# A quarter of the next norm's input, turned by DMA instead of TensorE at the ends of three feed-forward stages

## The chip, the cores and the metric

The kernel runs on one core of one Trainium2 chip. Times are device microseconds of one execution, from start to end; the median of three runs of the kernel before is 1848.39 us.

The engines are called by the profile's names: PE (TensorE, matmul), PEld (its weight loads), DVE (VectorE), ACT (ScalarE), POOL (GpSimd) and SP (SyncE, which only issues DMAs here).

## The reference

Two layers, each with three residual steps, on a float32 input of 512 tokens by 1024 channels:

```
x = x + 1/2 * SwiGLU(RMSNorm(x))        # FFN 1, inner width 2816
x = x + W_o(g_na * NA(h) W_na + g_f * FNet(h) W_f),  h = RMSNorm(x)
x = x + 1/2 * SwiGLU(RMSNorm(x))        # FFN 2

rms_norm(x, g) = x * rsqrt(mean(x * x) + 1e-6) * g
swiglu(x, w_in, w_out): g, u = split(x @ w_in); (silu(g) * u) @ w_out
```

A last RMSNorm ends it. What matters here is the border between one step and the next: the next step's products need the new x with channels on the partitions, multiplied by the norm's gain g.

## The kernel before

**Products.** Every float32 product is made of three matmuls. A number is split into a high part in the reduced fp32r format and the low rest; PE computes high times high (line 521), high weight times low activation (522) and low weight times high activation (524). The weight products run in a Strassen scheme: seven products of half-size blocks, numbered m = 1 to 7, stand for eight.

**Weights.** One list of weight blocks is walked through the whole program. SP loads a block (`raw`, 128x1024 or 128x512, line 148), up to 8 blocks ahead. Where a product wants the sum of two blocks, POOL adds the second by an accumulating DMA (line 158) or DVE adds it (line 172). ACT makes the high part `whi` (lines 199 and 194), DVE the low part `wlo` (lines 202 and 195), two blocks ahead of PE, in three buffers each.

**The end of a feed-forward stage.** The down projection is a list of 21 products (m, c), where c = 0, 1, 2 is the chunk of the inner width: m = 1 for c = 0 to 2, then m = 2 for c = 0 to 2, then 5, 6, 7, 3 of c = 0, the same of c = 1 and of c = 2, and last m = 4 for c = 0 to 2. The index i of the loop counts these; so i = 6 is product 5 of chunk 0, i = 13 is product 3 of chunk 1, i = 14, 15, 16 and 17 are products 5, 6, 7 and 3 of chunk 2, and i = 18 to 20 are product 4. The activations of product m are `c<m>h` (ACT, line 332) and `c<m>l` (DVE, line 333); some are combined first (DVE, line 779). The weight blocks of one product are its granules (two or three). When a product is complete over its chunks, DVE adds it to a quarter of x (`update`, line 785), and ACT sums the squares of that quarter for the next norm (`junk`, line 395).

**The next norm's input.** x is divided into four quarters: channel half i by token half j. `nxt.quad(i, j)` turns one. PE turns eight blocks of 128x128 into two PSUM banks `tr` (line 433), ACT multiplies by the gain from PSUM into `xr` (line 436, four of 128x256) and makes the high part `xh` (line 437), DVE the low part `xl` (line 438). Quarter (0, 0) of x is final behind the last m = 2 product, at i = 5; before, it is turned at i = 6. Quarters (1, 1) and (0, 1) are turned behind product 4 of chunk 0, and (1, 0) in the next stage.

**Turning by DMA.** The kernel has another way, which it uses for the gate's result: `words_apart` writes the 16-bit halves of a float32 block apart (`zs`, line 357, two ACT instructions of 128x1024), `turned_words` turns them by one transposing DMA from SP (`zt`, line 363), and `joined_words` puts the halves together again (line 376, two ACT instructions).

**Order.** What ACT, DVE and PE run is ordered by the compiler's list scheduler, except in blocks marked as manual. SP and POOL issue in program order, and each waits at a DMA whose buffer or source is not ready.

Of the kernel before, what the change touches and what calls it, by code (L numbers as in the profile page):

```python
# [9 lines left out]
F32 = mybir.dt.float32  # L10
# [4 lines left out]
AF = mybir.ActivationFunctionType  # L15
# [5 lines left out]
T = 512  # L21
# [70 lines left out]
def encoder_kernel(  # L92
    ctx: ExitStack, tc: tile.TileContext, xin, xtr, wst, gains, gfin, gbias, bias_in, dft, chan, ident_in, rot, out
):
    nc = tc.nc
    V, S, G, PE = nc.vector, nc.scalar, nc.gpsimd, nc.tensor
# [7 lines left out]
    dp = ctx.enter_context(tc.tile_pool(name="dp", bufs=2, space=bass.MemoryType.DRAM))  # L104
# [3 lines left out]
    def nm(s):  # L108
        uid[0] += 1
        return f"{s}_{uid[0]}"  # L110

    def slot(dt=F32, s="k", shape=(4, 256)):
        return kp.tile([P, *shape], dt, tag="k", name=nm(s), bufs=23)
# [12 lines left out]
    x = cp.tile([P, TB, D], F32, tag="x", name="x")  # L126
# [12 lines left out]
    class Raw:  # L139
# [3 lines left out]
        def load(self, parts=1):  # L143
            if self.t is None:
                self.t = raw_pool[0](self.n)
                for c in range(0, self.n, self.n // parts):
                    cs = slice(c, c + self.n // parts)
                    nc.sync.dma_start(out=self.t[:, cs], in_=wst[GRAN_AT[self.key]][:, cs])
                if self.plus:
                    gate = held.get(self.key)  # L150
                    if isinstance(gate, list):
                        gate.append(self)
                    else:
                        with tc.issue_after(gate) if gate else nullcontext():
                            self.summed()
# [48 lines left out]
                G.dma_start(out=t, in_=wst[GRAN_AT[self.then]][:, 0:n], accum_op=ALU.add)  # L204
            self.out = (hi, lo)

    held = {}

    def stage_items():
        items, st = [], 0  # L210
# [72 lines left out]
    class Stream:  # L283
# [32 lines left out]
        def next(self, ahead=AHEAD):  # L316
            self.prep(self.pos + 1 + ahead)
            it = self.items[self.pos]
            self.pos += 1
            return it.out  # L320
# [9 lines left out]
    def split(hi, lo, src, scale=None):  # L330
        if scale is None:
            S.activation(hi, src, AF.Copy)
            V.tensor_tensor(lo, src, hi.bitcast(F32), ALU.subtract)
            return
        S.activation(hi, src, AF.Copy, scale=scale)
        V.scalar_tensor_tensor(lo, src, scale, hi.bitcast(F32), ALU.mult, ALU.subtract)
# [15 lines left out]
    def words_apart(z):  # L352

        s = slot(U16, "zs", (2, 4, 2, P))
        words = z.bitcast(U16).rearrange("p b (q f h) -> p h q b f", q=4, h=2)
        for h in range(2):
            S.activation(s[:, h], words[:, h], AF.Copy)  # L357
        return s

    def turned_words(s):  # L360

        t = slot(U16, "zt", (2, 4, 256))
        nc.sync.dma_start_transpose(
            out=t.rearrange("p h q (b t) -> p (h q b) t", b=2), in_=s.rearrange("p h q b f -> p (h q b f)")
        )
        return t

    def apart(z):

        return turned_words(words_apart(z))  # L370

    def joined_words(to, t):

        to = to.bitcast(U16).rearrange("p i (t w) -> p w i t", w=2)
        for w in range(2):
            S.activation(to[:, w], t[:, w], AF.Copy)  # L376

    class Norm:
# [43 lines left out]
        def quad_high(self, i, j):  # L422

            self.tiles(i)
            js = slice(j * 256, (j + 1) * 256)
            hq, lq = self.h[i][:, :, js], self.l[i][:, :, js]
            raw = self.raw[i, j] = slot(F32, "xr")
            for k2 in range(2):
                tr = bank("tr").rearrange("p (a b) -> p a b", a=2)
                for k in range(2):  # L430
                    d = (4 * i + 2 * k2 + k) * P
                    for b in range(2):
                        PE.transpose(tr[:, k, b * P : (b + 1) * P], x[:, 2 * j + b, d : d + P], ident)
                for k in range(2):
                    kt = 2 * k2 + k
                    S.activation(raw[:, kt, :], tr[:, k, :], AF.Copy, scale=self.gain(4 * i + kt))
            S.activation(hq, raw, AF.Copy)
            return lambda: V.tensor_tensor(lq, raw, hq.bitcast(F32), ALU.subtract)

        def gain(self, kt):  # L440
            c = self.idx * DT + kt
# [186 lines left out]
    def stage_ffn(norm, nxt, late):  # L628
# [320 lines left out]
        if late or nxt.mix:  # L949
            tc.keep_in_program_order(S.activation(small("sq", 1), ones, AF.Sqrt))  # L950
        ps = {}
        for i, (m, c, _) in enumerate(steps):
            make(i)
            if i:
                make(i + 1)
            key = {6: 1, 4: 7}.get(m, m)
            if key not in ps:
                ps[key] = pair(f"o{key}")
            if m == 4 and c == 0 and nxt.mix:
                make(i + 2)  # L960
                ws.finish_stage()
                swap_pools(1)
            product(
                ps[key], made.pop(i), list(range(len(CHUNK[0][c]))), c == 0 and m in (1, 2, 3, 5, 7), c == 2,
                m in (4, 6), by_block=late and i == len(steps) - 1,
            )
            if i == 0:
                settle_at()
            if i == 3:
                turned.reverse()  # L970
                joined()
            if i == 5:
                joined()
            if m == 4 and c == 0 and not late:
                with tc.manual_schedule(engines={mybir.EngineType.DVE, mybir.EngineType.Activation}):
                    make(i + 2)
                    nxt.quad(1, 1)
                    if nxt.mix:
                        nxt.low01 = nxt.quad_high(0, 1)
                    else:  # L980
                        nxt.quad(0, 1)
            make(i + 2)
            if i == 6 and not late:
                nxt.quad(0, 0)
            if m == 4 and c == (0 if late else 1):
                update(ps[1], 1, 0, 1)
            if m == 4 and c == 0 and late:
                gf[0] = slot(F32, "gf", (D,))
                nc.sync.dma_start(out=gf[0], in_=bass.AP(tensor=gfin.tensor, offset=gfin.offset, ap=[[0, P], [1, D]]))
                ready = nxt.inverses(2)  # L990
                next(ready)
                next(ready)
                ends = nxt.terms()
            if m == 4 and c == 1 and late:
                for _ in ready:
                    pass
            if c < 2:
                continue
            if m == 1:
                update(ps[1], 0, 0, -1)  # L1000
            elif m == 2:
                update(ps[2], 0, 0, 1)
                nxt.squares(0, 0)
            elif m == 5:
                update(ps[5], 0, 1, 1)
                update(ps[5], 1, 1, -1)
            elif m == 6:
                update(ps[1], 1, 1, 1)
            elif m == 7:
                update(ps[7], 1, 1, 1)  # L1010
                nxt.squares(1, 1)
            elif m == 3:
                update(ps[1], 0, 1, -1)
                update(ps[3], 0, 1, 1)
                nxt.squares(0, 1)
                if late:
                    make(i + 3)
            elif late:
                with (
                    tc.issue_after(ws.items[-1].last.ins),  # L1020
                    tc.manual_schedule(engines={mybir.EngineType.DVE, mybir.EngineType.Activation}),
                ):
                    gained(2, 0)
                    gained(2, 1)
                    scaled(nxt, 2)
                    root = [nxt.inverse(b, *ends[b]) for b in range(2)]
                    update(ps[7], 1, 0, 1, (0,))
                    nxt.squares(1, 0, (0,))
                    next(root[0])
                    gained(3, 0)  # L1030
                    gained(3, 1)
                    scaled(nxt, 3)
                    gained(0, 0)
                    gained(1, 0)
                    update(ps[7], 1, 0, 1, (1,))
                    nxt.squares(1, 0, (1,))
                    next(root[1])
                    next(root[0])
                    next(root[0])
                    half_scaled(nxt, 0, 0)  # L1040
                    whole(nxt, 0, 1)
                    next(root[1])
                    next(root[1])
                    half_scaled(nxt, 1, 0)
                    whole(nxt, 1, 1)
            else:
                update(ps[7], 1, 0, 1)
                if not nxt.mix:
                    nxt.squares(1, 0)
                nxt.later((1, 0))  # L1050
# [982 lines left out]
```

## Time and profile before

| | us |
|---|---|
| runs of the kernel, median (lowest to highest of 3) | 1848.39 (1848.32 to 1849.78) |
| the profiled execution, its own time | 1848.74 |
| its span in the trace | 1847.0 |
| granted TensorE clock, mean | 0.998 |

A row of the timeline gives start, duration, engine, line, operation, what it writes and reads, the shape, how many of the same kind follow one another, and in brackets how long the engine had been idle before it and what released it. Times of rows are from the span's start. A row of several instructions gives the time from the first's start to the last's end. The next instruction of ACT or DVE may start about 0.1 us before the end that the row shows, and matmuls overlap by more, so spans between starts are used for sums. The three changed ends lie at 220 to 330 us (layer 0, FFN 1), 815 to 925 us (layer 0, FFN 2) and 1136 to 1245 us (layer 1, FFN 1).

### The profile page before, as it was taken

What the parts mean: (1) busy time and instruction counts of PE and PEld (TensorE: products, weight loads), DVE (VectorE), ACT (ScalarE), POOL (GpSimd) and SP (SyncE); (2) the same over time, 40 slices, a digit from 0 to 9 for tenths busy, and PEclk for the clock granted to TensorE, in tenths of its full rate; (3) what the DMA queues carried; (4) which work ended last, traced back from release to release, by engine and by line L of the source; (5) the groups of instructions that cost most, each with busy time, mean ns of one, the idle gap of its engine ahead of it and who ended that gap; (6) DMA issues with size and microseconds to landing.
All of it is one profiled execution on the core that took longest, in us unless ns stands there. A gap on an engine that the chain in (4) does not pass through costs nothing.

```text
span 1847.0 us, 24568 instructions
## 1 busy us (share of the span) xinstructions
PE 1835.7 (99%) x8850; PEld 1529.2 (83%) x8850; DVE 1602.6 (87%) x1942; ACT 1312.3 (71%) x1777; POOL 175.6 (10%) x215
## 2 busy tenths in 40 slices
PE   9999999999999999999999999999999999999998
PEld 7888888888888888888888888888888888888886
DVE  7878899786989987789998888997869899887898
ACT  6777875668676777787666778766776776777865
POOL 0001011100111010001010100101001101010010
PEclk9999999999999999999999999999999999999999
DMA  9898798933896789879888897989258966888695
GB/s 300 227 231 223 192 271 267 230 118 121 232 234 178 182 207 239 206 208 279 249 194 212 228 221 194 282 283 214 69 182 212 232 173 180 230 218 219 197 278 159
DMA packets 198378, 395.72 MB, mean 214 GB/s; under 512 B 103856, under 2 KB 103984, under 8 KB 198256
## 3 DMA queue, kind: packets, MB, share of 16 engines
q1 hardware_dynamic: 168912, 294.23, 49.9%
q0 software_dynamic: 28912, 99.38, 30.1%
q8 instruction: 69, 1.13, 0.2%
q10 hardware_dynamic: 432, 0.55, 0.1%
q14 instruction: 53, 0.43, 0.1%
HBM read 367.88 MB, written 2.11 MB: 200 GB/s over the span
## 4 chain that ended last, share of the span: by engine, by line
PE 94%; DVE 3%; issue 1%; DMA 1%; ACT 0%; POOL 0%; SPq 0%; DVEq 0%; ACTq 0%; POOLq 0%
PE A L521 10%; PE A L524 10%; PE A L522 10%; PE o L524 6%; PE o L521 6%; PE o L522 6%; PE B L521 5%; PE B L522 5%; PE B L524 5%; PE ps L326 4%; PE ps L327 3%; PE ps L328 3%; PE C L521 3%; PE C L522 3%; PE C L524 3%
## 5 line engine op out<-in xcount | busy, mean ns | idle before, releaser
L202 DVE TENSOR_TENSOR wlo<-raw,whi 128x1024 fp32r<-128x1024 f32 (+1 forms) x532 | 630.9, 1196 | 174.4 <-ACT whi L199 173.5
L199 ACT ACTIVATE whi<-raw 128x1024 fp32r<-128x1024 f32 (+1 forms) x532 | 544.0, 1033 | 263.4 <-PE A L522 53.6
L158 POOL DMA_DIRECT2D raw<-in_wst_dram x166 | 145.1, 898 | 1283.1 <-DMA raw<-in_wst_dram 530.5
L172 DVE TENSOR_TENSOR raw<-raw,raw 128x1024 f32<-128x1024 f32 (+1 forms) x148 | 177.0, 1196 | 2.0
L522 PE MATMUL A<-whi,xl 128*128 128x512 f32 x400 | 155.7, 389 | 0.0
L521 PE MATMUL A<-whi,xh 128*128 128x512 f32 x400 | 155.7, 389 | 0.0
L376 ACT ACTIVATE at<-zt 128x1024 uint16<-128x1024 uint16 (+2 forms) x96 | 110.3, 1166 | 15.1 <-DMA zt<-zs 15.0
L194 ACT ACTIVATE whi<-raw 128x1024 fp32r<-128x1024 f32 (+1 forms) x83 | 85.3, 1034 | 45.8 <-issue 12.5
L524 PE MATMUL A<-wlo,xh 128*128 128x512 f32 x400 | 115.0, 389 | 0.0
L195 DVE SCALAR_TENSOR_TENSOR wlo<-raw,whi 128x1024 fp32r<-128x1024 f32 (+1 forms) x83 | 98.6, 1198 | 13.1 <-ACT whi L194 13.1
L524 PEld LDWEIGHTS A<-wlo,xh 128*128 128x128 f32 x400 | 75.1, 188 | 15.5
L522 PEld LDWEIGHTS A<-whi,xl 128*128 128x128 f32 x400 | 75.1, 188 | 15.4
L521 PEld LDWEIGHTS A<-whi,xh 128*128 128x128 f32 x400 | 75.1, 188 | 15.4
L521 PE MATMUL C<-whi,xh 128*128 128x512 f32 x208 | 81.1, 390 | 0.2 <-ACT whi L199 0.2
L522 PE MATMUL C<-whi,xl 128*128 128x512 f32 x208 | 81.0, 389 | 0.0
L522 PE MATMUL B<-whi,xl 128*128 128x512 f32 x208 | 81.0, 389 | 0.0
L521 PE MATMUL B<-whi,xh 128*128 128x512 f32 x208 | 80.9, 389 | 0.0
L357 ACT ACTIVATE zs<-th 128x1024 uint16<-128x1024 uint16 x80 | 79.5, 1042 | 1.0 <-DVE th L766 0.9
L759 ACT ACTIVATE th<-sn,rh 128x512 f32<-128x512 f32 x80 | 55.1, 716 | 35.0 <-DVE sn L596 34.2
L591 ACT ACTIVATE sn<-A 128x512 f32<-128x512 f32 x104 | 59.2, 585 | 24.2 <-PE A L524 24.2
L524 PE MATMUL C<-wlo,xh 128*128 128x512 f32 x208 | 59.8, 389 | 0.0
L524 PE MATMUL B<-wlo,xh 128*128 128x512 f32 x208 | 59.8, 389 | 0.0
(429 smaller groups left out, 4686.6 us busy)
## 6 DMA issues: line engine op xcount, KB each, us to landing
raw<-in_wst_dram SPq DMA_DIRECT2D x468, 512.0 KB, 6.1
raw<-in_wst_dram POOLq DMA_DIRECT2D x176, 512.0 KB, 8.0
bm<-in_bias_dram SPq DMA_DIRECT2D x16, 512.0 KB, 4.1
raw<-in_wst_dram SPq DMA_DIRECT2D x30, 256.0 KB, 4.5
x<-in_xin_dram SPq DMA_DIRECT2D x4, 512.0 KB, 10.2
raw<-in_wst_dram POOLq DMA_DIRECT2D x8, 256.0 KB, 8.2
dft<-in_dft_dram POOLq DMA_DIRECT2D x8, 256.0 KB, 10.6
gb<-in_gbias_dram SPq DMA_DIRECT2D x4, 512.0 KB, 9.2
```

Of the source, the lines that this page charges most:

```text
L158: G.dma_start(out=self.t, in_=wst[GRAN_AT[self.plus]][:, 0 : self.n], accum_op=ALU.add)
L172: V.tensor_tensor(self.raw.t, self.raw.t, self.add.t, ALU.add)
L194: S.activation(hi, t, AF.Copy, scale=-1.0)
L195: self.last = V.scalar_tensor_tensor(lo, t, -1.0, hi.bitcast(F32), ALU.mult, ALU.subtract)
L199: S.activation(hi[:, cs], t[:, cs], AF.Copy)
L202: self.last = V.tensor_tensor(lo[:, cs], t[:, cs], hi[:, cs].bitcast(F32), ALU.subtract)
L326: PE.matmul(ps, lh, rh, start=start, stop=False, skip_group_check=again)
L357: S.activation(s[:, h], words[:, h], AF.Copy)
L376: S.activation(to[:, w], t[:, w], AF.Copy)
L521: PE.matmul(ps, lh, rh, start=start, stop=False, skip_group_check=again)
L522: PE.matmul(ps, ll, rh, start=False, stop=False, skip_group_check=again)
L524: PE.matmul(ps, lh, rl, start=False, stop=stop, skip_group_check=again)
```

## The change

At the three ends that another stage's norm follows (not at the last one), quarter (0, 0) of x is no longer turned by PE at i = 6. A generator with four steps takes its place:

- i = 13: `words_apart` of the quarter, two ACT instructions.
- i = 14: a small DMA from SP, `seen`, that reads sixteen numbers of the weight block that POOL's newest accumulating DMA wrote, and so waits for it; behind it in SP's order, the transposing DMA.
- i = 16: `joined_words` into `xr`, two ACT instructions.
- i = 17: four in-place multiplications by the gain (ACT, line 460 of the changed kernel) and the split into `xh` (ACT) and `xl` (DVE).

```diff
@@ class Raw, load
                 if self.plus:
+                    newest_sum[0] = self
                     gate = held.get(self.key)
...
-    held = {}
+    held, newest_sum = {}, [None]
...
+    def behind(raw):
+
+        seen = dp.tile([16], F32, tag="seen", name=nm("seen"))
+        to = bass.AP(tensor=seen.tensor, offset=seen.offset, ap=[[16, 1], [1, 16]])
+        return tc.issue_after(nc.sync.dma_start(out=to, in_=raw.t[0:1, 0:16]).ins)
...
+        def turned_quad(self, i, j):
+
+            js = slice(j * 256, (j + 1) * 256)
+            s = words_apart(x[:, 2 * j : 2 * j + 2, i * T : (i + 1) * T])
+            yield
+            with behind(newest_sum[0]):
+                t = turned_words(s)
+            yield
+            self.tiles(i)
+            raw = self.raw[i, j] = slot(F32, "xr")
+            joined_words(raw, t)
+            yield
+            for k in range(4):
+                S.activation(raw[:, k, :], raw[:, k, :], AF.Copy, scale=self.gain(4 * i + k))
+            split(self.h[i][:, :, js], self.l[i][:, :, js], raw)
+            yield
...
         ps = {}
+        quad00 = nxt.turned_quad(0, 0)
         for i, (m, c, _) in enumerate(steps):
...
             make(i + 2)
-            if i == 6 and not late:
-                nxt.quad(0, 0)
+            if i in (13, 14, 16, 17) and not late:
+                next(quad00)
```

What the scheduler makes of it on ACT, at the end of layer 0, FFN 1, from the weight split of product 4, chunk 0, first granule, on. Before (`whi_2652` and `whi_2668` belong to chunk 0 of product 4, `whi_2702` and `whi_2706` to chunk 1, `whi_2710` to chunk 2):

```order
L199 ACTIVATE whi_2652<-raw_2493 128x1024
L332 ACTIVATE c4h_2685<-at_1814 128x1024
L199 ACTIVATE whi_2668<-raw_2517 128x512
L395 ACTIVATE junk_2648,ssq_181<-x 128x512
L395 ACTIVATE junk_2650,ssq_181<-x 128x512
L199 ACTIVATE whi_2702<-raw_2536 128x1024
L332 ACTIVATE c4h_2698<-at_2074 128x1024
L199 ACTIVATE whi_2706<-raw_2563 128x1024
L395 ACTIVATE junk_2693,ssq_181<-x 128x512
L199 ACTIVATE whi_2710<-raw_2581 128x1024
```

The same place of the changed kernel, where `whi_2645` and `whi_2661` belong to chunk 0 and `whi_2701` to chunk 1:

```order
L200 ACTIVATE whi_2645<-raw_2474 128x1024
L383 ACTIVATE xr_2636<-zt_2545 128x1024 x2
L402 ACTIVATE junk_2641,ssq_181<-x 128x512
L200 ACTIVATE whi_2661<-raw_2501 128x512
L402 ACTIVATE junk_2643,ssq_181<-x 128x512
L333 ACTIVATE c4h_2678<-at_1814 128x1024
L460 ACTIVATE xr_2636<-xr_2636,gn 128x256 x4
L333 ACTIVATE c4h_2697<-at_2074 128x1024
L333 ACTIVATE xh_2634<-xr_2636 128x4x256
L402 ACTIVATE junk_2692,ssq_181<-x 128x512
L402 ACTIVATE junk_2694,ssq_181<-x 128x512
L200 ACTIVATE whi_2701<-raw_2520 128x1024
```

The first weight split of chunk 1 stood five rows behind that of chunk 0; now the joins, the scalings, `xh` and both c4h are ahead of it. The end of layer 1, FFN 1, has the same row order. At the end of layer 0, FFN 2, the order differs. Before, from the split of product 3, chunk 2, second granule (`whi_8005`), on; `whi_8034` and `whi_8052` are product 4, chunk 0, and `whi_8084` is chunk 1:

```order
L199 ACTIVATE whi_8005<-raw_7725 128x1024
L199 ACTIVATE whi_8034<-raw_7871 128x1024
L332 ACTIVATE c4h_8069<-at_7194 128x1024
L199 ACTIVATE whi_8052<-raw_7895 128x512
L395 ACTIVATE junk_8028,ssq_5468<-x 128x512
L395 ACTIVATE junk_8030,ssq_5468<-x 128x512
L199 ACTIVATE whi_8084<-raw_7914 128x1024
```

And of the changed kernel, where `whi_7992` is that of product 3, `whi_8026` and `whi_8044` are product 4, chunk 0, and `whi_8082` is chunk 1:

```order
L200 ACTIVATE whi_7992<-raw_7705 128x1024
L383 ACTIVATE xr_8015<-zt_7922 128x1024 x2
L200 ACTIVATE whi_8026<-raw_7851 128x1024
L402 ACTIVATE junk_8020,ssq_5467<-x 128x512
L402 ACTIVATE junk_8022,ssq_5467<-x 128x512
L200 ACTIVATE whi_8044<-raw_7878 128x512
L333 ACTIVATE c4h_8061<-at_7193 128x1024
L460 ACTIVATE xr_8015<-xr_8015,gn 128x256 x4
L200 ACTIVATE whi_8082<-raw_7897 128x1024
L333 ACTIVATE xh_8013<-xr_8015 128x4x256
```

Here the split of chunk 1 (`whi_8082`) has only the joins and the scalings put ahead of it, and `xh` stays behind it.

On SP, at the end of layer 0, FFN 1, the rows before are loads alone:

```order
L148 DMA raw_2493<-in_wst_dram 128x1024
L148 DMA raw_2517<-in_wst_dram 128x512
L148 DMA raw_2536<-in_wst_dram 128x1024
L148 DMA raw_2563<-in_wst_dram 128x1024
L148 DMA raw_2581<-in_wst_dram 128x1024
```

In the changed kernel the small read and the transposing DMA stand between them (`raw_2474`, `raw_2501` and `raw_2520` are the three blocks of product 4 that are `raw_2493`, `raw_2517` and `raw_2536` above):

```order
L148 DMA raw_2474<-in_wst_dram 128x1024
L373 DMA seen_2543<-raw_2413 1x16
L148 DMA raw_2501<-in_wst_dram 128x512
L148 DMA raw_2520<-in_wst_dram 128x1024
L364 DMA_TRANSPOSE zt_2545<-zs_2498 128x16x128
L148 DMA raw_2551<-in_wst_dram 128x1024
L148 DMA raw_2569<-in_wst_dram 128x1024
```

So every load from `raw_2501` on now stands behind the read that waits for POOL's last accumulation, and from `raw_2551` on behind the transposing DMA too. On PE the eight transposes are gone at three places and nothing else is moved.

## The prediction

> **What bounds the kernel now.** I read the busy shares first, then the chain that ended last, then the rows of the removed work, and last the windows and timelines round one changed place.
>
> ```profile
> PE 1835.7 (99%) x8850; PEld 1529.2 (83%) x8850; DVE 1602.6 (87%) x1942; ACT 1312.3 (71%) x1777; POOL 175.6 (10%) x215
> PE 94%; DVE 3%; issue 1%; DMA 1%; ACT 0%; POOL 0%; SPq 0%; DVEq 0%; ACTq 0%; POOLq 0%
> L433 PE MATMUL tr<-ident,x x160: 270/272/273, 254.2 to 1535.3; 128*128 128x128 f32 x160
> 250.00:255.00 5.00, 5.00 (x29) 4.21 (x27) 5.00 (x9) 3.76 (x7) 1.05 (x2) 1.00 0.97 235
> 305.00:310.00 5.00, 4.79 (x21) 3.43 (x20) 5.00 (x6) 3.43 (x4) 0.11 (x1) 1.00 0.95 347
> ```
>
> TensorE is busy 99% of the span and carries 94% of the chain. So an instruction that leaves TensorE shortens the program, provided its next operands are there in time. The third row lists the transposes; the change removes 24 of those 160 (8 at each of three FFN ends). The last two rows are windows of the first FFN's end (window; its length; then the busy time of PE, PEld, DVE, ACT, POOL; clock; DMA share; GB/s). Behind the removed transposes PE is full at a granted clock of 1.00; but DVE is full as well, the DMA engines are at 0.97, and in 305 to 310 PE has lost 0.21 us. The other engines have hardly any cover there, so the change is not judged by PE's share alone.
>
> **What is removed.** In the first FFN's end:
>
> ```profile
> 253.97 0.39 PE L524 MATMUL o<-wlo,c5h 128*128 128x512 f32 x1
> 254.20 1.03 PE L433 MATMUL tr<-ident,x 128*128 128x128 f32 x8
> 254.99 0.49 PE L521 MATMUL o<-whi,c6h 128*128 128x512 f32 x1
> 255.31 0.40 PE L522 MATMUL o<-whi,c6l 128*128 128x512 f32 x1
> ```
>
> Products start every 0.23 us (253.97 to 254.20). Eight transposes hold the next product back by 254.99 - 254.20 = 0.79 us, and the product behind them takes 0.32 us until the next start, 0.09 too long. That is 0.88 us a place, 2.6 us for three, 0.14% of the run: **the whole possible gain is under the 0.2%** (3.7 us) that a measurement of this kernel can tell from no change.
>
> **Where the first gain goes.** At the first FFN's end the 0.88 us have to survive the stretch up to product 3 of chunk 2:
>
> ```profile
> 277.83 2.01 ACT L199 ACTIVATE whi<-raw 128x1024 fp32r<-128x1024 f32 x2 [1.75 <-DMA raw<-in_wst_dram]
> 278.93 1.22 DVE L202 TENSOR_TENSOR wlo<-raw,whi 128x1024 fp32r<-128x1024 f32 x1 [1.06 <-ACT whi L199]
> 307.64 1.21 PE L524 MATMUL o<-wlo,c3h 128*128 128x512 f32 x4 [0.21 <-DVE wlo L202]
> ```
>
> A weight lands late before 277.83, DVE starts again at 278.93 and has no gap from there on until PE waits for its wlo at 307.64. The same DVE work lies in that stretch after the change (the moved xl subtraction leaves it at the front, before the gap, and comes back behind it). So PE, 0.88 us ahead, waits 0.88 us longer at 307.64, unless the landing moves ahead too: a load starts when a buffer comes free, so by at most the same 0.88 us. I call that lead d, from 0 to 0.88 us, and take the middle, 0.45, since no row decides it.
>
> **What is added on ACT, and when.** The two cuts of x into 16-bit words (zs) cost little:
>
> ```profile
> L357 ACT ACTIVATE zs<-th x80: 1036/1042/1061, 70.4 to 1737.9; 128x1024 uint16<-128x1024 uint16 x80
> 287.97 1.04 ACT L199 ACTIVATE whi<-raw 128x1024 fp32r<-128x1024 f32 x1
> 290.49 1.06 ACT L199 ACTIVATE whi<-raw 128x1024 fp32r<-128x1024 f32 x1 [1.48 <-DVE raw L172]
> ```
>
> They are 2 x 1.04 us in the row order behind the whi of 287.97, where ACT idles 1.48 us waiting for DVE; the rest delays operands that DVE, full of older work, takes later. Cost: nothing. The dear part is where the rejoining, scaling and splitting stand. In ACT's rows of the first and third changed end, everything from the joined words to the split xh stands ahead of the first weight split (whi) of product 4, chunk 1. Before:
>
> ```profile
> 306.57 2.01 ACT L199 ACTIVATE whi<-raw 128x1024 fp32r<-128x1024 f32 x2 [2.81 <-DVE raw L172]
> 308.48 1.04 ACT L332 ACTIVATE c4h<-at 128x1024 fp32r<-128x1024 f32 x1
> 309.43 0.62 ACT L199 ACTIVATE whi<-raw 128x512 fp32r<-128x512 f32 x1
> 310.23 0.63 ACT L395 ACTIVATE junk<-x 128x512 bf16<-128x512 f32 x1 [0.18 <-DVE x L785]
> 310.86 0.61 ACT L395 ACTIVATE junk<-x 128x512 bf16<-128x512 f32 x1
> 311.47 1.05 ACT L199 ACTIVATE whi<-raw 128x1024 fp32r<-128x1024 f32 x1
> 312.42 1.04 ACT L332 ACTIVATE c4h<-at 128x1024 fp32r<-128x1024 f32 x1
> 317.36 0.49 PE L521 MATMUL o<-whi,c4h 128*128 128x512 f32 x1
> ```
>
> The whi of 311.47 ends at 312.52; PE uses it at 317.36, so it has 4.84 us to spare. Durations of the new rows, by the nearest rows of the same kind:
>
> ```profile
> 242.82 2.58 ACT L376 ACTIVATE at<-zt 128x1024 uint16<-128x1024 uint16 x2
> 245.25 1.04 ACT L199 ACTIVATE whi<-raw 128x1024 fp32r<-128x1024 f32 x1
> 913.17 1.54 ACT L436 ACTIVATE xr<-tr,gn 128x256 f32<-128x256 f32 x4
> 914.74 1.06 ACT L437 ACTIVATE xh<-xr 128x1024 fp32r<-128x1024 f32 x1
> 915.71 1.55 ACT L436 ACTIVATE xr<-tr,gn 128x256 f32<-128x256 f32 x4
> 917.14 1.08 ACT L199 ACTIVATE whi<-raw 128x1024 fp32r<-128x1024 f32 x1
> ```
>
> Start to start: two joins 2.43 us, four scalings 1.43 (915.71 to 917.14; 1.57 at 913.17), one xh 0.97. In-place scalings are not in the trace; these rows read PSUM and write the same shape, and I bound the four by 1.2 and 1.6. From 306.57 the changed order then gives: two whi 1.91, joins 2.43, junk 0.61, whi of 512 columns 0.62, junk 0.61, c4h 0.95, scalings 1.43, c4h 0.95, xh 0.97, two junk 1.22, and the whi itself 1.05; the sum is 12.75, so it ends at 319.3 - d instead of 312.5. PE waits from 317.36 to 319.3: **+1.95 - d** against before, whatever lead PE had. The same queue brings the c4h of chunk 1 to 312.8 from 308.5, and with it DVE's c4l, the x updates and PE's 16 transposes at 315.70, which stand ahead of that product; these come about a microsecond late and then fall inside the same wait.
>
> The third changed end (layer 1, FFN 1) has the same row order:
>
> ```profile
> 1221.60 2.01 ACT L199 ACTIVATE whi<-raw 128x1024 fp32r<-128x1024 f32 x2 [2.80 <-DVE raw L172]
> 1232.83 0.49 PE L521 MATMUL o<-whi,c4h 128*128 128x512 f32 x1
> ```
>
> 1221.60 + 12.75 = 1234.35 against 1232.83: **+1.5 - d**. In the second end (layer 0, FFN 2) the whi of product 4, chunk 1, stands ahead of xh and of two junks:
>
> ```profile
> 901.78 2.01 ACT L199 ACTIVATE whi<-raw 128x1024 fp32r<-128x1024 f32 x2 [2.81 <-DVE raw L172]
> 908.01 0.39 PE L521 MATMUL o<-whi,c4h 128*128 128x512 f32 x1
> 913.76 0.49 PE L521 MATMUL o<-whi,c4h 128*128 128x512 f32 x1
> ```
>
> From 901.78: whi 0.95, joins 2.43, whi of product 4 chunk 0 to 906.2 (PE wants it at 908.01 - 0.88 = 907.1), junks 1.22, whi 0.62, c4h 0.95, scalings 1.43, whi to 911.4 (PE wants it at 912.9). Both are in time, by 0.9 and 1.5 us, so the full **-0.88** stays.
>
> **The queues that are passed.** SP gets the small read `seen` behind the last accumulated weight, then two weight loads, then the transposing DMA. Nothing else joins POOL's queue.
>
> ```profile
> 297.66 1.06 ACT L199 ACTIVATE whi<-raw 128x1024 fp32r<-128x1024 f32 x1 [0.80 <-DMA raw<-in_wst_dram]
> L363 SPq DMA_TRANSPOSE zt<-zs x44: 1317/3365/5361, 72.5 to 1738.9; - x44
> DMA to landing us min/median/max: 3.2/5.5/7.4
> DMA to landing us min/median/max: 3.4/6.4/11.3
> ```
>
> The last accumulation has landed by 297.6 (first row). SP stands still until then, issues `seen`, two loads and the transpose by about 299, and the words land 3.2 to 7.4 us later (third row: the 44 transposes of the same tile size), at 302 to 306.5; ACT comes to the joins at 308.5. So the wait is hidden by 2 us or more. The loads behind `seen` land in 3.4 to 11.3 us (last row, SP's weight loads of 285 to 325), by 310 at worst, and the first is wanted at 309.43: cost nothing, to +1 if the worst falls there. The transposing issue itself holds SP for 1.3 to 5.4 us (second row), to 304; the load behind it, for the second weight of product 4, chunk 1, lands by 315.5, and ACT now comes to it at 319.
>
> A rule of the Trainium skill speaks against this swap. "VectorE: DVE Perf Modes", section "Rules for kernel authors", says to turn 128x128 blocks on TensorE where PSUM can be the destination and by the crossbar DMA otherwise, and its section on the three transpose paths gives 390 ns and 1309 ns a block. As an estimate from that page, 16 blocks in a row would be 20.9 us on the DMA. The trace disagrees in part: eight f32 transposes cost PE 0.88 us, and a DMA of 16 blocks lands within 7.4 us.
>
> **Sum.** Against the profiled execution's 1848.74 us (its span of 1847.0 and 1.74 around it): +1.95 - 0.88 + 1.5 - 2d = +2.6 - 2d, which is +2.6 with d = 0, +0.8 with d = 0.88 and +1.7 in the middle. That profiled run lies 0.35 us above the median 1848.39, so the median goes to about **1850.0**, with 1849 to 1851.5 as this case's own range (scalings at 1.2 or 1.6 move it by 0.5 at each FFN1 end).
>
> **The rivals.**
> - *The whole gain.* ACT's queue runs further ahead than I hold, or PE takes the late whi within its slack: 1848.39 - 2.6 = 1845.8. For it: PE is full almost everywhere. Against it: 12.75 us of queue against 10.8 us of room. Chance 0.12.
> - *The change does nothing for the end.* The freed 0.88 us turn into waits for weights at all three ends, and the longer queue is just covered: 1848.4. For it: in both windows above DVE is full. Against: at the second end PE and DVE showed no stall. Chance 0.10.
> - *Late words, slower.* The joins stand at the head of ACT's queue with every weight split behind them. From a landing of 9.9 us on (308.5 - 298.6), each microsecond is one more on PE at the first and third end, and at the second from 0.9 us later. At 11.3 us, the longest landing of SP in that stretch, this gives +1.4 and +1.4 and +0.5, with d = 0 a sum of +5.9: 1854.3; with half of that delay 1852.6. For it: the DMA engines are at 0.95 and more in the windows above, and the transpose stands behind the accumulation's landing, so it is late with it. Against: no transpose of 44 took over 7.4. Chance 0.18. A smaller form of it at d = 0 stays in my own case.
> - *A transpose whose blocks go one by one.* If each of the 16 blocks took 1.3 us, the shortest time that the row above gives for a whole transposing issue, the words would land 21 us behind 298.6, the joins would wait from 308.5 to 319.6, and each end would lose about 11 us more: 1882 to 1884. Against: the same 7.4 us. Chance 0.01. That is what the rule named above would make of it.
> - *More than the gain.* PE's lead also frees weight buffers earlier, and the stall of 0.21 and its like vanish: under 1844.7. Chance 0.04.
>
> **How the numbers follow.** My case has 0.55, the whole gain 0.12, nothing 0.10, late words and serial blocks 0.19, more than the gain 0.04. Faster by over 0.2% (under 1844.7): 0.05. Slower by over 0.2% (over 1852.1): 0.19. Within: 0.76. The range runs from the whole gain, 1845.8, to 1853.5, which takes in most of the late words' case; it leaves out 0.04 below and about 0.1 above. The likeliest number is 1850.0.
>
> **What the profile after would show.** Right: no tr row of eight behind product 5 of chunk 0; the word transposes land before ACT's joins, which have no wait for zt; at the first and third end, PE waits 1 to 2 us at the first product of product 4, chunk 1, released by ACT's whi, and none at the second. Wrong: ACT sits idle at the joins with zt as releaser (late words); PE shows no wait there and the ends come 0.9 us earlier each (whole gain); PE waits longer for wlo at product 3, but not at product 4 (nothing).

## The result, and the profile after

| | us |
|---|---|
| kernel before, median of 11 runs | 1848.34 (1846.98 to 1850.53) |
| changed kernel, median of 11 runs | 1853.08 (1851.36 to 1854.88) |
| ratio | 1.0025, 95% interval 1.0016 to 1.0034 |
| the changed kernel's profiled execution | 1854.1, span 1852.3 |

The change makes the kernel 4.7 us slower. Two executions far above all others (2635.82 us in experiment 4, 2479.87 us of the kernel before) are not in the ratios below. The page's busy times of the changed kernel:

```profile
PE 1837.0 (99%) x8826; PEld 1526.2 (82%) x8826; DVE 1602.9 (87%) x1942; ACT 1324.3 (71%) x1789; POOL 176.0 (10%) x215
```

PE has 24 matmuls fewer and DVE and POOL as many as before; ACT has 12 instructions and 12 us more. At the place of the first removal, PE's timeline is now without a break:

```profile
253.90 0.39 PE L548 MATMUL o<-wlo,c5h 128*128 128x512 f32 x1
254.12 0.39 PE L545 MATMUL o<-whi,c6h 128*128 128x512 f32 x1
```

PE's first removal is there; the loss comes later. ACT at the first end, from the weight splits of product 3 and product 4, chunk 0, to that of product 4, chunk 1:

```profile
305.26 2.01 ACT L200 ACTIVATE whi<-raw 128x1024 fp32r<-128x1024 f32 x2 [2.81 <-DVE raw L173]
307.17 2.58 ACT L383 ACTIVATE xr<-zt 128x1024 uint16<-128x1024 uint16 x2
309.61 0.60 ACT L402 ACTIVATE junk<-x 128x512 bf16<-128x512 f32 x1
...
312.30 1.69 ACT L460 ACTIVATE xr<-xr,gn 128x256 f32<-128x256 f32 x4
313.90 1.04 ACT L333 ACTIVATE c4h<-at 128x1024 fp32r<-128x1024 f32 x1
314.84 1.04 ACT L333 ACTIVATE xh<-xr 128x1024 fp32r<-128x1024 f32 x1
...
317.02 2.94 ACT L200 ACTIVATE whi<-raw 128x1024 fp32r<-128x1024 f32 x3
```

ACT has no idle time from 305.26 on: the last row's whi is late because it stands last in a full queue. The joins at 307.17 wait for nothing, so the words were in time. PE beside it:

```profile
314.40 2.08 PE L440 MATMUL tr<-ident,x 128*128 128x128 f32 x16
318.11 0.50 PE L545 MATMUL o<-whi,c4h 128*128 128x512 f32 x1 [1.62 <-ACT whi L200]
```

PE stands still for 1.62 us at the first product of product 4, chunk 1, and ACT's whi ends that. At the third end the same, and ahead of it more. ACT and PE there:

```profile
1191.39 1.06 ACT L200 ACTIVATE whi<-raw 128x1024 fp32r<-128x1024 f32 x1 [2.95 <-DMA raw<-in_wst_dram]
1195.16 2.01 ACT L200 ACTIVATE whi<-raw 128x1024 fp32r<-128x1024 f32 x2 [1.76 <-DMA raw<-in_wst_dram]
1223.89 2.00 ACT L200 ACTIVATE whi<-raw 128x1024 fp32r<-128x1024 f32 x2 [2.81 <-DVE raw L173]
1235.63 2.94 ACT L200 ACTIVATE whi<-raw 128x1024 fp32r<-128x1024 f32 x3
```

```profile
1224.96 1.20 PE L548 MATMUL o<-wlo,c3h 128*128 128x512 f32 x4 [0.67 <-DVE wlo L203]
1236.73 0.50 PE L545 MATMUL o<-whi,c4h 128*128 128x512 f32 x1 [1.62 <-ACT whi L200]
```

DVE's timeline of the third end shows what the two late weights of ACT's first rows did:

```profile
1192.48 1.23 DVE L203 TENSOR_TENSOR wlo<-raw,whi 128x1024 fp32r<-128x1024 f32 x1 [1.81 <-ACT whi L200]
1193.62 1.22 DVE L173 TENSOR_TENSOR raw<-raw,raw 128x1024 f32<-128x1024 f32 x1
1196.25 1.23 DVE L203 TENSOR_TENSOR wlo<-raw,whi 128x1024 fp32r<-128x1024 f32 x1 [1.42 <-ACT whi L200]
```

Before, DVE had no gap there. Now it idles 3.2 us, and the queue of ACT that begins with product 3's last split starts at 1223.89 instead of 1221.60.

At the second end, where the splits of chunk 1 stay ahead of xh, PE has no such wait:

```profile
911.06 1.04 ACT L200 ACTIVATE whi<-raw 128x1024 fp32r<-128x1024 f32 x1
912.01 1.04 ACT L333 ACTIVATE xh<-xr 128x1024 fp32r<-128x1024 f32 x1
```

It is not free of loss all the same: DVE waits for ACT's whi and c4h there (0.24 us ahead of 906.89, 0.25 us ahead of 909.58), and PE, behind DVE, gives back 0.83 us.

How far PE leads or lags the trace before is read by matching the same matmul in both and taking the difference of their starts (us, negative is ahead): the first matmul of product 4, chunk 1, at 317.36 before and at 318.11 here makes +0.75. "Start" is ahead of the first removal: what stands there is the scatter of two executions.

| execution | start | past removal 1 | product 4, c 0 | c 1 | next stage | ahead of end 2 | past removal 2 | past end 2 | past removal 3 | product 4, c 0 | c 1 | next stage | mixer's middle |
|---|---|---|---|---|---|---|---|---|---|---|---|---|---|
| changed | -0.07 | -1.01 | -1.29 | +0.75 | +0.74 | +0.17 | -0.76 | +0.07 | -0.90 | +1.87 | +3.93 | +3.93 | +5.56 |
| changed, second trace | -0.37 | -1.31 | -0.05 | +2.05 | +2.05 | +1.44 | +0.50 | +0.50 | -0.47 | +2.65 | +4.73 | +4.73 | +6.23 |

(The middle of the mixer is at 1350 us of the trace before; the second trace is an experiment below.) Each removal gives 0.93 or 0.94 us. The first end gives back 2 us at chunk 1 of product 4, the third end 2.8 to 3.1 us ahead of product 4 and 2.1 at it.

### The profile page after: what moved, and what is told of

The parts are those of the page before. It is cut to its first block, busy times and chain, and to the rows that moved or that the text cites. A ratio compares the mean times of both kernels' runs of the same rounds, so it can differ in the third digit from the quotient of the medians.

```text
span 1852.3 us, 24543 instructions
## 1 busy us (share of the span) xinstructions
PE 1837.0 (99%) x8826; PEld 1526.2 (82%) x8826; DVE 1602.9 (87%) x1942; ACT 1324.3 (71%) x1789; POOL 176.0 (10%) x215
```

## The experiments

Two theories. **Queue theory**: the loss is where the scheduler puts the added work on ACT (and DVE): weight splits stand behind it. **DMA theory**: the small read holds SP, and the transposing DMA takes time of the DMA engines, so weights are late. Times are medians; ratios are against the kernel before on the same chip.

**1. The split one step later.**

```diff
-            if i in (13, 14, 16, 17) and not late:
+            if i in (13, 14, 16, 18) and not late:
```

> The scaling and split of the turned quarter are issued at i = 18 instead of 17, so ACT makes the weight split of product 4, chunk 1, ahead of them; joins, words and DMAs stay. Queue theory (ACT's order at two ends, 1.9 and 2.1 us of PE wait on whi): those two waits vanish, the 2.7 us of wlo waits at the end of layer 1, FFN 1, stay: 1848.5 to 1849.5 us. DMA theory (the small read that holds SP and the transposing DMA make weights late): no change, 1852 to 1854 us.

Measured: 1857.75 us, ratio 1.0047 (1.0035 to 1.0060): slower still, which neither theory expected. The wait at product 4 is gone, and a larger one stands at the next stage's first products:

```profile
330.45 0.49 PE L545 MATMUL A<-whi,xh 128*128 128x512 f32 x1 [1.01 <-ACT xh L333]
331.83 0.50 PE L546 MATMUL A<-whi,xl 128*128 128x512 f32 x1 [0.88 <-DVE xl L334]
```

The scheduler now put xh behind the next stage's other quarter, and that stage begins with it. PE lost 4.1 us at the first and 4.0 us at the third of these borders. The two waits, with one matmul between them, are only 2.3 us of that (at 0.23 us a product the first was due at 329.28 and started at 330.45, the second was due at 330.68 and started at 331.83). Most of the rest is TensorE's clock. Windows of that trace:

```profile
331.00:332.00 1.00, 0.17 (x1) 0.17 (x2) 0.97 (x2) 1.00 (x2) 0.00 (x0) 1.00 1.03 422
333.00:334.00 1.00, 1.00 (x4) 0.78 (x3) 1.00 (x2) 0.93 (x1) 0.00 (x0) 0.50 1.02 410
337.00:338.00 1.00, 1.00 (x6) 0.84 (x5) 0.96 (x4) 0.13 (x1) 0.00 (x0) 1.00 0.00 0
```

Behind the waits PE is full, but the granted clock is 0.50 for about 3.4 us, which costs half of that, 1.7 us; products start every 0.43 us there (333.03, 333.45, 333.88). The third border shows the same, and so do both borders of experiment 3. Behind the single wait of 1.62 us for whi in the changed kernel the clock stays at 1.00. So 1.7 us at each border of experiments 1 and 3 are not waiting.

The place in ACT's queue sets the waits, and the work has a due time on both sides.

**2. DVE's order put back, ACT's left.** Product 4's combinations are issued where the kernel before runs them.

```diff
+        def four(c):
+            if c not in fours:
+                fours[c] = comb(part(1, 0, c), part(1, 0, c), part(0, 0, c), ALU.subtract)
+            return fours[c]
...
+            if i in {8: 0, 11: 1, 15: 2} and not late:
+                four({8: 0, 11: 1, 15: 2}[i])
```

> The changed kernel with only DVE's order put back: product 4's combinations of chunks 0, 1, 2 are issued at i = 8, 11, 15, where the kernel before runs them; scaling and split stay at i = 17. Queue theory: the ACT waits of about 2 us at both FFN 1 ends stay, the wlo waits at the end of layer 1, FFN 1, shrink from 2.7 to under 1: about 1851 us. DMA theory: 1852 to 1854 us.

Measured: 1851.86 us, ratio 1.0021 (1.0012 to 1.0030). The waits on whi stay (+2.1 us at both ends). At the third end PE lost 1.9 us ahead of product 4, against 2.8 and 3.1 in the two traces of the changed kernel: less, but not under 1. The intervals of this ratio and the changed kernel's overlap, so what the order of the combinations costs is not settled by time.

**3. Both.**

> Split at i = 18 and combinations pinned, all else as in the changed kernel. Queue theory: no wait of PE on whi at product 4 and hardly any on wlo, so most of 2.6 us of removed transposes stays: 1846 to 1847.5 us, faster than the kernel before. DMA theory: 1852 to 1854 us.

Measured: 1857.52 us, ratio 1.0047 (1.0034 to 1.0060), with the same waits for xh and xl and the same low clock as in the first (4.1 us in all at each border). Ahead of the first of them PE was 0.9 us ahead of its start and had kept the whole gain up to there.

**4. The words alone.** The quarter is still turned by PE; the cuts, the small read and the transposing DMA are issued, and the words are not used.

```diff
-            if i in (13, 14, 16, 17) and not late:
+            if i == 6 and not late:
+                nxt.quad(0, 0)
+            if i in (13, 14) and not late:
                 next(quad00)
```

> The kernel before with its quarter still turned by PE, and beside it the two word cuts on ACT, the small read and the transposing DMA of the change, whose result is not read. Queue theory: two ACT instructions in idle time, 1848 to 1849 us. DMA theory: the whole loss and the removed transposes besides, 1852 to 1856 us.

Measured: 1849.28 us, ratio 1.0003 (0.9994 to 1.0012). In its trace PE's lag is -0.4 us behind the first end and changes by no more than 0.1 us at the two others; between them, in layer 0's mixer, it moves by 0.5 us and back. The DMA theory, which put the whole loss here, falls: SP's halt and the transposing DMAs cost nothing that the trace shows, and at most 2.2 us by the interval.

**5. The split at its due place.** Scaling and split stand in the block that runs in program order behind product 4, chunk 0; once with the combinations pinned, once without.

```diff
                 with tc.manual_schedule(engines={mybir.EngineType.DVE, mybir.EngineType.Activation}):
+                    next(quad00)
                     make(i + 2)
                     nxt.quad(1, 1)
...
-            if i in (13, 14, 16, 17) and not late:
+            if i in (13, 14, 16) and not late:
                 next(quad00)
```

> Scaling and split of the turned quarter stand at the head of the block that runs in program order behind product 4 of chunk 0; ACT then makes both weight splits of chunk 1 and the first of chunk 2 ahead of them, and xh still ahead of the next stage's quarters. Combinations of product 4 pinned. Queue theory: no wait of PE on whi at product 4 and none on xh at the next stage's first product: 1846 to 1847.5 us. DMA theory (late weights): 1851 to 1854 us.

> The same without pinning the combinations. Queue theory: the ACT waits are gone; whatever DVE's later combinations cost stays at layer 1, FFN 1: 1847 to 1849 us, 1 to 2 us over the pinned one. If the combinations cost nothing: equal to the pinned one within 0.5 us. DMA theory: 1851 to 1854 us.

Measured: 1849.43 us, ratio 1.0002 (0.9994 to 1.0011), and 1849.29 us, ratio 1.0007 (0.9998 to 1.0016). ACT at the first end, pinned:

```profile
313.77 1.05 ACT L200 ACTIVATE whi<-raw 128x1024 fp32r<-128x1024 f32 x1
...
318.79 1.69 ACT L460 ACTIVATE xr<-xr,gn 128x256 f32<-128x256 f32 x4
320.51 1.06 ACT L333 ACTIVATE xh<-xr 128x1024 fp32r<-128x1024 f32 x1
```

The whi of chunk 1 is at 313.77 and PE waits for no whi at either end, nor for xh. The order on ACT was worth about 3.7 us, 1853.08 less 1849.4. But nothing is faster than before: the removed 2.8 us are not in the time. Pinned or not makes no difference here, so the combinations are not the cause of what is left.

**6. The removal alone.** ACT scales x itself, with no transposes, words or DMAs.

```diff
+                S.activation(raw[:, kt, :], v, AF.Copy, scale=self.gain(4 * i + kt))   # v: 128x256 of x
...
             if i == 6 and not late:
-                nxt.quad(0, 0)
+                nxt.quad_unturned(0, 0)
```

> The kernel before with the eight transposes of quarter (0, 0) left out at i = 6 at the three ends: ACT scales x itself into xr, so the turning is left out; no word, no DMA, no other order. It measures what the removal alone can give. Queue theory: 1845.8 to 1846.5 us (2.0 to 2.6 us less). If PE's lead is eaten by weights and DVE at every end: 1848 to 1848.7 us.

Measured: 1849.80 us, ratio 1.0005 (0.9996 to 1.0013). So even the bare removal gives nothing. Its trace: PE gains 0.94 us at each of the three places, and loses 0.7, 3.6 and 0.6 us again before the end of the stage. At the second end two weights are late, DVE stands still and PE then waits for it. ACT's rows, DVE's rows, then rows of the waits from 815 to 910 us (who waited for whom: us in total, times, longest; PEld's waits hold PE back too):

```profile
872.98 1.06 ACT L199 ACTIVATE whi<-raw 128x1024 fp32r<-128x1024 f32 x1 [3.52 <-DMA raw<-in_wst_dram]
876.83 1.06 ACT L199 ACTIVATE whi<-raw 128x1024 fp32r<-128x1024 f32 x1 [2.79 <-DMA raw<-in_wst_dram]
874.07 1.23 DVE L202 TENSOR_TENSOR wlo<-raw,whi 128x1024 fp32r<-128x1024 f32 x1 [3.34 <-PE o L532]
877.92 1.23 DVE L202 TENSOR_TENSOR wlo<-raw,whi 128x1024 fp32r<-128x1024 f32 x1 [1.49 <-ACT whi L199]
```

```profile
ACT whi L199 <- DMA raw<-in_wst_dram: 6.5, 3, 3.5
PEld o L534 <- DVE wlo L202: 3.5, 7, 1.1
PE o L534 <- DVE wlo L202: 0.7, 1, 0.7
```

The first DVE row names PE as its releaser, but ACT's whi, late by its load, ended at 874.04, just ahead of it. In this trace PE does not gain because DVE, once stopped by a late weight, has no slack up to product 3 of chunk 2; experiment 8 puts that to the test.

**7. The changed kernel once more**, for its trace.

> The changed kernel once more, for its trace. Queue theory: about 2 us of PE wait on whi at the first product of product 4, chunk 1, at both FFN 1 ends, as in the first trace. If the 2.7 us of wlo waits at layer 1, FFN 1, and the 1.4 us in the mixer behind it come from that execution alone, they are smaller or elsewhere here; if from the order, the wlo waits stay within 1 us.

Measured: 1856.38 us in one run. The PE waits on whi are 1.62 us again at the first end (PE then starts at 319.38), and the wlo waits and the mixer's loss come back (3.1 and 1.5 us, the table above). So they are not of one execution.

**8. Slack for DVE.** Two of DVE's weight additions an end are left out, in the kernel of experiment 5 (pinned), in the kernel before as a control, and in that without the transposes.

```diff
-                V.tensor_tensor(self.raw.t, self.raw.t, self.add.t, ALU.add)
+                if not self.unsummed:
+                    V.tensor_tensor(self.raw.t, self.raw.t, self.add.t, ALU.add)
...
                     add(d, None if dma else b)
+                    items[-1].unsummed = name("a") == "oa" and idx == 2
```

> The kernel of the pinned sums with the split inside the ordered block, and DVE's two weight additions of product 3, chunk 2, left out at the ends that make them on DVE (their weights are loaded but not added, so that part of the sum is left out). Theory that the removed transposes are lost because DVE, behind a late weight, has no slack up to product 3 of chunk 2: with 2.3 us less DVE work ahead of that product the lead of 0.9 us an end stays, 2 to 2.6 us under the control that leaves out the same additions in the kernel before. Theory that the gain goes elsewhere (ACT, the joins, the DMAs): within 0.7 us of that control.

> The control: the kernel before with the same two weight additions a stage left out. Its own waits at product 3 were 0.2 us at one end, so both theories expect 1847.5 to 1848.8 us.

> The control without the eight transposes at i = 6: ACT writes zeros of the same shape into xr, so the turning is left out, and so are the two weight additions. DVE theory: 2 to 2.6 us under the control. Other theory: within 0.7 us of it, as the removal alone was within 1 us of the kernel before.

Measured: 1846.43 us for the turn by DMA, 1847.38 for the control, 1846.14 for the removal alone; ratios against the kernel before 0.9991 (0.9982 to 1.0000), 0.9992 (0.9984 to 1.0001) and 0.9987 (0.9978 to 0.9996). The sizes, 0.95 and 1.24 us under the control, lie between the two expectations and inside the intervals. The traces tell more. PE's lead over the control's trace:

| execution | start | past removal 1 | end 1 over | past removal 2 | past end 3 | 1775 us | 1830 us |
|---|---|---|---|---|---|---|---|
| turn by DMA, no sums | +0.81 | -0.13 | -0.13 | -1.05 | -2.01 | -2.01 | -0.69 |
| removal alone, no sums | +0.26 | -0.68 | -0.68 | -0.76 | -1.62 | -1.64 | +0.68 |

With DVE's slack, nothing is lost at the three ends by these two traces: the first kernel goes from +0.81 to -2.01, all of 3 x 0.94; the second gains as much at each end and loses 0.9 us in a mixer between them. The third end shows the same across all traces. DVE's idle time there, from the removal to product 3 of chunk 2, beside what PE loses from behind the removal to product 4 (us):

| third end | DVE idle | PE loses |
|---|---|---|
| before; experiments 4 and 9 (turned by PE) | 0.0; 0.2, 0.2 | 0.0; 0.0, 0.0 |
| changed, first and second trace | 3.2, 3.3 | 2.8, 3.1 |
| experiments 1, 2, 3 | 1.7, 2.4, 1.2 | 1.2, 1.9, 0.7 |
| experiment 5, pinned and not | 2.4, 1.8 | 1.9, 1.3 |
| removal alone (6) | 1.1 | 0.6 |
| no sums: turn by DMA, removal alone | 1.4, 1.9 | 0.0, 0.0 |

In every trace without the transposes and with DVE's additions PE loses DVE's idle time less 0.2 to 0.6 us, and where DVE has 2.3 us less to do, stops of 1.4 and 1.9 us cost nothing. The slack differs by end: at the second, DVE idles 2.6 us in the changed kernel's first trace and PE loses only 0.1 us up to product 4. So the DVE theory holds at these ends. But 1.3 and 2.3 us are lost at the last FFN's end, which was not changed. ACT and DVE there, in the removal alone, and the window of that end:

```profile
1785.35 1.06 ACT L201 ACTIVATE whi<-raw 128x1024 fp32r<-128x1024 f32 x1 [3.45 <-DMA raw<-in_wst_dram]
1786.44 1.23 DVE L204 TENSOR_TENSOR wlo<-raw,whi 128x1024 fp32r<-128x1024 f32 x1 [2.31 <-ACT whi L201]
1790.06 1.23 DVE L204 TENSOR_TENSOR wlo<-raw,whi 128x1024 fp32r<-128x1024 f32 x1 [1.26 <-ACT whi L201]
```

```profile
1765.00:1815.00 50.00, 49.10 (x212) 39.11 (x211) 45.78 (x46) 26.05 (x28) 7.80 (x9) 1.00 1.02 281
```

PE has lost 0.9 us in these 50, where the control loses none, again behind late weights. That the lead itself causes this is not shown: with PE's transposes kept at the third end the lag against the kernel before moves from 1775 to 1830 us by +0.6 (experiment 4), -0.8 (the control) and -0.8 us (experiment 9), so part of it is scatter.

**9. One end only.** The turn by DMA only at the end of layer 0, FFN 2, with the split inside the ordered block.

```diff
+                    if not nxt.mix:
+                        next(quad00)
...
-            if i in (13, 14, 16) and not late:
+            if i == 6 and nxt.mix:
+                nxt.quad(0, 0)
+            if i in (13, 14, 16) and not late and not nxt.mix:
                 next(quad00)
```

> The turn by DMA only at the end of layer 0, FFN 2, with the split inside the ordered block; the two FFN 1 ends as before. Queue theory: no new wait; PE's lead of 0.9 us stays there if DVE has its slack (no gap of DVE in the trace before): 1847.9 us, at best 0.05% under the kernel before and not to be told from it by time; the trace shows how much of 0.9 us is left at 930 us.

Measured: 1846.58 us, ratio 0.9988 (0.9979 to 0.9996): the one version that does all its work and whose interval lies below 1, though only just, and one such among a dozen ratios proves little. PE's lead goes from 1.24 to 2.18 us at the removal and is still 2.18 at 930 us and at 1350 us, so 0.94 us are the change's; the other 1.24 us were there ahead of the changed place and belong to the execution.

## Why the prediction was right, and where it was off

The sign, the first place and the mechanism (ACT's queue ahead of the split of product 4, chunk 1) were right. The size was not: 1.6 us were forecast and 4.7 came, 0.25% where most of the chance lay on less than 0.2%. The case's own range, 1849 to 1851.5, was missed. 1853.08 lies in the wide range, up to 1853.5, only because that was stretched for late words, which did not come; that it holds is luck.

- **What is removed**: 0.88 us a place were worked out, 0.93 or 0.94 measured at all three.
- **Where the first gain goes**: right in its cause (late weight, then a full DVE), and the lead d was wider than I bounded it. The queue's first row started at 305.26 in the first trace and 306.53 in the second, against 306.57: d is 1.31 and 0.04, where I had 0 to 0.88.
- **ACT's queue**: 12.75 us were added up; from 305.26 to the end of the first whi (317.02 and one whi of 1.05) are 12.8, and from 1223.89 to 1236.7 also 12.8. The in-place scaling, which I bounded by 1.2 and 1.6, takes 1.60 to the next row.
- **The second end**: no wait of PE on whi, as worked out. Of the gain, 0.1 us was left in the first trace, where DVE waited for ACT's later whi and c4h, and 0.94 in the second. The prediction looked at PE's need of whi there, and not at DVE's.
- **The queues that are passed**: right. The joins had no wait for words at any end of the changed kernel's first trace, and the trace of experiment 4 shows no cost of SP's halt and the DMAs. With that the rivals of late words and of blocks one by one fall, and the rule of the Trainium skill ("VectorE: DVE Perf Modes", "Rules for kernel authors") that prefers TensorE holds here for another reason than its price of the DMA: the ACT work that comes with the words. (A slip in the first of these rivals: half of its delay is 0.7 us, within the second end's margin of 0.9 us, so its 1852.6 should have been 1852.4.)
- **The third end, the step that failed**: "1221.60 + 12.75 = 1234.35 against 1232.83: +1.5 - d". The start was taken from the trace before and only allowed to be earlier. In the first trace it was 2.29 us later, because DVE stopped 3.2 us for late weights where it had no gap before; in the second it was 3.10 us later (1224.70; 0.47 of that from ahead of this end), with 3.3 us of stops. The term was +1.05 with the middle d, and measured +3.9 and +4.3 (from +0.04 to +3.93 and from +0.47 to +4.73).
- **A term that was missing**: in the middle of layer 1's mixer the changed kernel loses 1.6 and 1.5 us more. The orders of ACT, DVE and PE there are the same as before behind the third end's last rows.

The whole-gain rival was wrong for a reason that I had only at the first end: experiments 6 and 8 show that the removed 2.8 us are taken back where DVE, stopped by late weights, has no slack.

**What stays open.** Why weights are late in one execution and not in another is not settled. The table of experiment 8 ties PE's loss at the third end to DVE's stops, from 1.1 to 3.3 us in all eight traces without the transposes there and with the additions, but not the stops to a cause. That DVE has one combination and the xl less ahead of that place, and so reaches the weights sooner, is a possible one; pinning the combination did not settle it. The mixer's loss appears in both traces of the changed kernel and not in those of experiments 1, 2 and 5; no run isolates its cause. The changed kernel without the small read was not tried.

## What to carry to other kernels

Ask of work taken off the busiest engine whether the engine next to it has any slack up to the next shared wait: here 0.94 us came free on PE three times and was lost, since DVE was full behind a late weight. Do not read a loss of PE as waiting alone: look at the granted clock behind the wait too. Work that replaces it on another engine has a due time and a place in that engine's queue: read the order that the scheduler makes, and add the queue up from the row that starts it. When that start hangs on a transfer, its later side belongs in the bounds as well as its earlier one.

## What the runs showed of the hardware

Four in-place scalings of 128x256 on ACT take 1.60 us start to next start, where four that read PSUM took 1.43 and 1.57. The transposing DMA holds SP's queue for 3.77 us (third end), and the read behind the last accumulation was let go only at 1213.12:

```profile
1213.12 0.26 SPq L373 DMA_DIRECT2D seen<-raw  x1
1214.39 3.77 SPq L364 DMA_TRANSPOSE zt<-zs  x1
```

Neither shows in the time of experiment 4. Two stalls of PE close together (1.01 and 0.88 us, one matmul between them) were followed by about 3.4 us at a granted clock of 0.50, at all four borders of experiments 1 and 3; a single stall of 1.62 us was not. No run here shows where the limit lies. Single executions of one kernel differ by more than the effects here (1846.98 to 1850.53 for the kernel before), so leads were read inside a trace, place by place, and only then compared with the medians.
